# LayerNorm of x + residual on one core: loads two tiles at a time, stores issued by GpSimd instead of ScalarE

## The chip, the core and the metric

The kernel runs on one core of a Trainium2 chip. The engines that matter are VectorE (DVE), ScalarE (ACT), GpSimd (POOL, used here only to issue DMAs) and SyncE (SP, used only to issue DMAs), and the 16 DMA engines that the core's DMA queues share. TensorE does no work. The metric is the device time of one execution in microseconds (us); before the change the median of 4 runs is 265.06 us (264.94 to 265.14).

## The reference

```python
x, residual: (16, 1024, 512) float32    gamma, beta: (512,) float32
z = x + residual
mean = np.mean(z, axis=-1, keepdims=True)
var = np.var(z, axis=-1, keepdims=True)
out = gamma * (z - mean) / np.sqrt(var + eps) + beta
```

These are 16384 rows of 512 numbers. Each of x, residual and the output is 33.55 MB in float32, so that at least 100.7 MB cross the memory interface, whatever the kernel does.

## The kernel before

Each of the 128 partitions holds 128 consecutive rows, and the kernel goes through them in tiles of `_R = 4` rows per partition: a tile is 128 x 4 x 512 numbers, 1 MB in float32. The loop that makes the list of tiles halves the last one, so that there are 31 tiles of four rows and 2 tiles of two rows.

The work on tile i is cut into stages. `emit_loads` brings x by a DMA from SP's queue (tile `zt`) and residual by a DMA from POOL's queue (tile `rt`), which turns it into bf16 on the way. `emit_sums` has DVE add the residual in place and collect the sum of each row (L94, four instructions), and has ACT square the sum and collect the sum of squares (L101, four). `emit_m2`, `emit_var`, `emit_sqrt` and `emit_rstd` are small instructions on 4 numbers per partition, on DVE but for the square root on ACT. `emit_norm` has ACT write (z - mean) / std as bf16 into `ut` (L165, four). `emit_fin` has DVE multiply by gamma (`wt`, L178) and add beta (`ot`, L183), and issues the store of the tile, from ACT's queue (L188).

The main loop is a software pipeline written out by hand: in its turn i it emits the loads up to tile i + 11, the norm of tile i - 4, the sums of tile i, and the end (`emit_fin`) of tile i - 5:

```python
for i in range(n_t + 5):
    for k in range(10):
        emit_loads(i + 2 + k)
    emit_norm(i - 4)
    emit_sqrt(i - 2)
    emit_sums(i)
    emit_m2(i)
    emit_fin(i - 5)
    emit_rstd(i - 3)
    emit_var(i - 1)
```

A scheduler then fixes an order for each engine; each engine takes its instructions in that order, and an instruction that waits holds up all behind it on its engine. The number of buffers sets how far one engine may run ahead of another: 12 tiles for x (`_XB`), 12 for residual (`_RB`), 4 for the output (`_OB`). An x buffer comes free when the norm of its tile is done, a residual buffer when the sums of its tile are done, an output buffer when its store has landed. Beside that, the DMAs that SP and ACT issue share eight semaphores (DMAHW0 to DMAHW7), taken in turn, and those that POOL issues have eight others (DMASW0 to DMASW7): a DMA whose semaphore is still in use waits at its issue until the earlier DMA with it has landed.

Of the kernel before, what the change touches and what calls it, by code (L numbers as in the profile page):

```python
# [7 lines left out]

_R = 4
_XB = 12  # L10
_RB = 12
_OB = 4
_CAST_R = True
_STORE_Q = "act"


@with_exitstack
def kernel(
    ctx: ExitStack,
    tc: tile.TileContext,  # L20
    x: bass.AP,
    residual: bass.AP,
    gamma: bass.AP,
    beta: bass.AP,
    eps: bass.AP,
    out: bass.AP,
):
    nc = tc.nc
    P = nc.NUM_PARTITIONS

    f32 = mybir.dt.float32
    bf16 = mybir.dt.bfloat16
    AT = mybir.ActivationFunctionType
    OP = mybir.AluOpType

    x_f = x.flatten_outer_dims()
    r_f = residual.flatten_outer_dims()
    o_f = out.flatten_outer_dims()
    N, D = x_f.shape
    assert D <= 512  # L40

    inv_d = 1.0 / float(D)
    eps_f = float(eps)

    n_rows = N // P
    tiles = []
    r0 = 0
    while r0 < n_rows:
        rem = n_rows - r0
        R = _R if rem > _R else max(_R // 2, 1)  # L50
        R = min(R, rem)
        tiles.append((r0, R))
        r0 += R
    n_t = len(tiles)

    x_v = x_f.rearrange("(p r) d -> p r d", p=P)
    r_v = r_f.rearrange("(p r) d -> p r d", p=P)
    o_v = o_f.rearrange("(p r) d -> p r d", p=P)

    consts = ctx.enter_context(tc.tile_pool(name="consts", bufs=1))  # L60
    xz = ctx.enter_context(tc.tile_pool(name="xz", bufs=_XB))
    rl = ctx.enter_context(tc.tile_pool(name="rl", bufs=_RB))
    mids = ctx.enter_context(tc.tile_pool(name="mids", bufs=3))
    outs = ctx.enter_context(tc.tile_pool(name="outs", bufs=_OB))
    stats = ctx.enter_context(tc.tile_pool(name="stats", bufs=6))
    junk = ctx.enter_context(tc.tile_pool(name="junk", bufs=1, space=bass.MemoryType.PSUM))

    st = {}

    def emit_loads(i):  # L70
        if i >= n_t or i in st:
            return
        r0, R = tiles[i]
        zt = xz.tile([P, _R, D], f32, name=f"zt{i}", tag="zt")[:, :R]
        nc.sync.dma_start(out=zt, in_=x_v[:, r0 : r0 + R])  # L75
        if _CAST_R:
            rt = rl.tile([P, _R, D], bf16, name=f"rt{i}", tag="rt")[:, :R]
            nc.gpsimd.dma_start(out=rt, in_=r_v[:, r0 : r0 + R])  # L78
        else:
            rt = rl.tile([P, _R, D], f32, name=f"rt{i}", tag="rt")[:, :R]  # L80
            nc.sync.dma_start(out=rt, in_=r_v[:, r0 : r0 + R])
        st[i] = dict(zt=zt, rt=rt)

    sq_junk = junk.tile([P, D], f32, name="sq_junk")

    def emit_sums(i):
        if i >= n_t or i < 0:
            return
        s = st[i]
        r0, R = tiles[i]  # L90
        zt, rt = s["zt"], s["rt"]
        sums = stats.tile([P, _R], f32, name=f"sums{i}", tag="sums")
        for j in range(R):
            nc.vector.scalar_tensor_tensor(  # L94
                out=zt[:, j], in0=zt[:, j], scalar=0.0, in1=rt[:, j],
                op0=OP.add, op1=OP.add,
                accum_out=sums[:, j : j + 1],
            )
        ssq = stats.tile([P, _R], f32, name=f"ssq{i}", tag="ssq")
        for j in range(R):  # L100
            nc.scalar.activation(  # L101
                out=sq_junk, in_=zt[:, j], func=AT.Square,
                accum_out=ssq[:, j : j + 1],
            )
        s["sums"] = sums
        s["ssq"] = ssq

    def emit_m2(i):
        if i >= n_t or i < 0:
            return  # L110
        s = st[i]
        r0, R = tiles[i]
        m2 = stats.tile([P, _R], f32, name=f"m2{i}", tag="m2")
        nc.vector.scalar_tensor_tensor(  # L114
            out=m2[:, :R], in0=s["sums"][:, :R], scalar=-inv_d,
            in1=s["sums"][:, :R], op0=OP.mult, op1=OP.mult,
        )
        s["m2"] = m2

    def emit_var(i):  # L120
        if i >= n_t or i < 0:
            return
        s = st[i]
        r0, R = tiles[i]
        varn = stats.tile([P, _R], f32, name=f"varn{i}", tag="varn")
        nc.vector.tensor_tensor(  # L126
            out=varn[:, :R], in0=s["ssq"][:, :R], in1=s["m2"][:, :R], op=OP.add
        )
        s["varn"] = varn

    def emit_sqrt(i):
        if i >= n_t or i < 0:
            return
        s = st[i]
        r0, R = tiles[i]
        stdv = stats.tile([P, _R], f32, name=f"stdv{i}", tag="stdv")
        nc.scalar.activation(  # L137
            out=stdv[:, :R], in_=s["varn"][:, :R], func=AT.Sqrt, bias=eps_t,
            scale=inv_d,
        )  # L140
        s["stdv"] = stdv

    def emit_rstd(i):
        if i >= n_t or i < 0:
            return
        s = st[i]
        r0, R = tiles[i]
        rstd = stats.tile([P, _R], f32, name=f"rstd{i}", tag="rstd")
        nc.vector.reciprocal(out=rstd[:, :R], in_=s["stdv"][:, :R])  # L149
        cc = stats.tile([P, _R], f32, name=f"cc{i}", tag="cc")  # L150
        nc.vector.scalar_tensor_tensor(  # L151
            out=cc[:, :R], in0=s["sums"][:, :R], scalar=-inv_d, in1=rstd[:, :R],
            op0=OP.mult, op1=OP.mult,
        )
        s["rstd"] = rstd
        s["cc"] = cc

    def emit_norm(i):
        if i >= n_t or i < 0:
            return  # L160
        s = st[i]
        r0, R = tiles[i]
        ut = mids.tile([P, _R, D], bf16, name=f"ut{i}", tag="ut")
        for j in range(R):
            nc.scalar.activation(  # L165
                out=ut[:, j], in_=s["zt"][:, j], func=AT.Identity,
                bias=s["cc"][:, j : j + 1], scale=s["rstd"][:, j : j + 1],
            )
        s["ut"] = ut

    def emit_fin(i):
        if i >= n_t or i < 0:
            return
        s = st[i]
        r0, R = tiles[i]
        ut = s["ut"][:, :R]
        wt = mids.tile([P, _R, D], bf16, name=f"wt{i}", tag="wt")[:, :R]
        nc.vector.tensor_tensor(  # L178
            out=wt, in0=ut, in1=gamma_bf.unsqueeze(1).to_broadcast((P, R, D)),
            op=OP.mult,  # L180
        )
        ot = outs.tile([P, _R, D], f32, name=f"ot{i}", tag="ot")
        nc.vector.tensor_tensor(  # L183
            out=ot[:, :R], in0=wt,
            in1=beta_f.unsqueeze(1).to_broadcast((P, R, D)), op=OP.add,
        )
        eng = nc.scalar if _STORE_Q == "act" else nc.gpsimd
        eng.dma_start(out=o_v[:, r0 : r0 + R], in_=ot[:, :R])  # L188
        del st[i]

    emit_loads(0)
    emit_loads(1)

    gamma_f = consts.tile([P, D], f32)
    nc.sync.dma_start(out=gamma_f, in_=gamma.unsqueeze(0).to_broadcast((P, D)))  # L195
    beta_f = consts.tile([P, D], f32)
    nc.sync.dma_start(out=beta_f, in_=beta.unsqueeze(0).to_broadcast((P, D)))  # L197
    gamma_bf = consts.tile([P, D], bf16)
    nc.vector.tensor_copy(out=gamma_bf, in_=gamma_f)  # L199
    eps_t = consts.tile([P, 1], f32)  # L200
    nc.vector.memset(eps_t, eps_f)  # L201

    for i in range(n_t + 5):
        for k in range(10):
            emit_loads(i + 2 + k)
        emit_norm(i - 4)
        emit_sqrt(i - 2)
        emit_sums(i)
# [4 lines that stand above are left out]
# [35 lines left out]
```

## Time and profile before

| | before |
|---|---|
| median of 4 runs | 265.06 us |
| the profiled execution, its time | 265.22 us |
| its span, first to last instruction | 263.3 us |
| DVE busy | 203.2 us (77%) |
| ACT busy | 182.6 us (69%) |
| POOL busy (issue of DMAs) | 17.8 us (7%) |
| read from memory / written to it | 67.63 MB / 33.55 MB |
| the chain that ended last | DMA 61%, ACT 16%, DVE 13% |

A queue q1 of the profile carries the loads of x (SP), q0 the loads of residual (POOL), and q10 the stores (ACT). The sizes that the profile gives are those of what is written, so that q0 shows half of what it reads: it reads float32 and writes bf16. A chain of waits is read backwards from the last instruction, and its shares say which kind of work the end hung on, not that this work was at its limit the whole time.

### The profile page before, as it was taken

To read this page: it belongs to the slowest core of one execution; us is meant where nothing else is said; L and a number is where in the kernel's file an instruction comes from. 1 tells how busy PE (TensorE), PEld (TensorE's weight loads), DVE (VectorE), ACT (ScalarE), POOL (GpSimd) and SP (SyncE) were. 2 spreads that over 40 slices of the span, in tenths; PEclk is the share of its full clock that TensorE was granted. 3 is DMA by queue.
4 is the path that set the end of the run, shared out by engine and by line. 5 is a ranking of instruction groups with operands and counts; after the bars stand their busy time and mean duration, and the time that the engine had idled before them with its cause. 6 is when DMAs were issued, how large, how long until landed. Compare 5 with 4: busy or idle time off the path is not lost.

```text
span 263.3 us, 1203 instructions
## 1 busy us (share of the span) xinstructions
DVE 203.2 (77%) x456; ACT 182.6 (69%) x419; POOL 17.8 (7%) x37
## 2 busy tenths in 40 slices
DVE  0354696792959998699989878888898589976893
ACT  1386689564354842999987885777770699999950
POOL 6010011000100000000000000000000000000000
DMA  7999999999999999999999999999999998433756
GB/s 251 251 265 313 317 316 340 339 351 349 325 353 321 353 350 327 348 350 352 359 350 347 351 361 350 349 356 355 350 348 356 371 382 355 205 159 159 299 236 261
DMA packets 14552, 84.48 MB, mean 321 GB/s; under 512 B 1616, under 2 KB 1616, under 8 KB 6608
## 3 DMA queue, kind: packets, MB, share of 16 engines
q1 hardware_dynamic: 5040, 34.08, 32.4%
q0 software_dynamic: 4752, 16.78, 31.7%
q10 hardware_dynamic: 4752, 33.56, 30.5%
q14 instruction: 8, 0.07, 0.1%
HBM read 67.63 MB, written 33.55 MB: 384 GB/s over the span
## 4 chain that ended last, share of the span: by engine, by line
DMA 61%; ACT 16%; DVE 13%; issue 7%; ACTq 1%; SPq 1%; DVEq 0%
DMA zt<-in_x_dram 61%; ACT ut L165 8%; ACT sq_junk L101 7%; DVE ot L183 4%; DVE zt L94 4%; DVE wt L178 3%; ACTq L188 1%; ACT stdv L137 1%; DVE varn L126 1%; DVE cc L151 0%; DVE rstd L149 0%; SPq L75 0%; SPq L197 0%; SPq L195 0%; DVE m L114 0%
## 5 line engine op out<-in xcount | busy, mean ns | idle before, releaser
L101 ACT ACTIVATE sq_junk<-zt 128x512 f32<-128x512 f32 x128 | 75.0, 586 | 58.1 <-DVE cc L151 24.8
L94 DVE SCALAR_TENSOR_TENSOR zt<-zt,rt 128x512 f32<-128x512 f32 x128 | 81.4, 688 | 43.8 <-DMA zt<-in_x_dram 32.5
L165 ACT ACTIVATE ut<-zt,cc,rstd 128x512 bf16<-128x512 f32 x128 | 98.7, 799 | 3.3 <-DVE cc L151 3.3
L183 DVE TENSOR_TENSOR ot<-wt,beta_f 128x2048 f32<-128x2048 bf16 (+1 forms) x33 | 73.4, 2225 | 0.1
L178 DVE TENSOR_TENSOR wt<-ut,gamma_bf 128x2048 bf16<-128x2048 bf16 (+1 forms) x33 | 39.2, 1188 | 6.5 <-ACT ut L165 6.3
L78 POOL DMA_DIRECT2D rt<-in_residual_dram x33 | 17.6, 541 | 145.6 <-DMA rt<-in_residual_dram 124.0
L101 ACT ACTIVATION_READ_ACCUMULATOR sq_junk<-zt 128x1 f32 x128 | 23.9, 187 | 0.0
L137 ACT ACTIVATE stdv<-varn,eps_t 128x4 f32<-128x4 f32 (+1 forms) x33 | 9.4, 284 | 7.5 <-DVE varn L126 7.5
L94 DVE DVE_READ_ACCUMULATOR zt<-zt,rt 128x1 f32 x128 | 10.5, 82 | 0.0
L126 DVE TENSOR_TENSOR varn<-ssq,m 128x4 f32<-128x4 f32 (+1 forms) x33 | 5.2, 156 | 3.1 <-ACT sq_junk L101 3.1
L149 DVE RECIPROCAL rstd<-stdv 128x4 f32<-128x4 f32 (+1 forms) x33 | 5.6, 170 | 0.8 <-ACT stdv L137 0.8
L114 DVE SCALAR_TENSOR_TENSOR m<-sums 128x4 f32<-128x4 f32 (+1 forms) x33 | 5.2, 159 | 0.8
L101 ACT ACT_TABLE_LOAD x1 | 1.3, 1283 | 5.7 <-DMA zt<-in_x_dram 5.7
L151 DVE SCALAR_TENSOR_TENSOR cc<-sums,rstd 128x4 f32<-128x4 f32 (+1 forms) x33 | 5.1, 156 | 0.0
L137 ACT ACT_TABLE_LOAD x1 | 1.3, 1283 | 0.0
L201 DVE MEMSET eps_t<- 128x1 f32 x1 | 0.1, 59 | 0.8 <-PEq L229 0.8
L199 DVE CAST gamma_bf<-gamma_f 128x512 bf16<-128x512 f32 x1 | 0.4, 422 | 0.0
L229 POOL MEMSET const-float32-0.0<- 128x1 f32 x1 | 0.1, 99 | 0.2 <-issue 0.2
L229 POOL MEMSET const-bfloat16-1.0<- 128x1 bf16 x1 | 0.1, 102 | 0.0
L229 POOL MEMSET const-float32-1.0<- 128x1 f32 x1 | 0.1, 99 | 0.0
L229 POOL MEMSET const-uint8-127<- 128x1 uint8 x1 | 0.1, 99 | 0.0
## 6 DMA issues: line engine op xcount, KB each, us to landing
zt<-in_x_dram SPq DMA_DIRECT2D x31, 1024.0 KB, 30.5
out_dram<-ot ACTq DMA_DIRECT2D x31, 1024.0 KB, 11.4
rt<-in_residual_dram POOLq DMA_DIRECT2D x31, 512.0 KB, 51.7
zt<-in_x_dram SPq DMA_DIRECT2D x2, 512.0 KB, 25.1
out_dram<-ot ACTq DMA_DIRECT2D x2, 512.0 KB, 2.9
rt<-in_residual_dram POOLq DMA_DIRECT2D x2, 256.0 KB, 56.8
gamma_f<-in_gamma_dram SPq DMA_DIRECT2D x1, 256.0 KB, 12.4
beta_f<-in_beta_dram SPq DMA_DIRECT2D x1, 256.0 KB, 15.6
```

Of the source, the lines that this page charges most:

```text
L78: nc.gpsimd.dma_start(out=rt, in_=r_v[:, r0 : r0 + R])
L94: nc.vector.scalar_tensor_tensor(out=zt[:, j], in0=zt[:, j], scalar=0.0, in1=rt[:, j], op0=OP.add, op1=OP.add, accum_out=sums[:, j : j + 1],)
L101: nc.scalar.activation(out=sq_junk, in_=zt[:, j], func=AT.Square, accum_out=ssq[:, j : j + 1],)
L114: nc.vector.scalar_tensor_tensor(out=m2[:, :R], in0=s["sums"][:, :R], scalar=-inv_d, in1=s["sums"][:, :R], op0=OP.mult, op1=OP.mult,)
L126: nc.vector.tensor_tensor(out=varn[:, :R], in0=s["ssq"][:, :R], in1=s["m2"][:, :R], op=OP.add)
L137: nc.scalar.activation(out=stdv[:, :R], in_=s["varn"][:, :R], func=AT.Sqrt, bias=eps_t, scale=inv_d,)
L149: nc.vector.reciprocal(out=rstd[:, :R], in_=s["stdv"][:, :R])
L151: nc.vector.scalar_tensor_tensor(out=cc[:, :R], in0=s["sums"][:, :R], scalar=-inv_d, in1=rstd[:, :R], op0=OP.mult, op1=OP.mult,)
L165: nc.scalar.activation(out=ut[:, j], in_=s["zt"][:, j], func=AT.Identity, bias=s["cc"][:, j : j + 1], scale=s["rstd"][:, j : j + 1],)
L178: nc.vector.tensor_tensor(out=wt, in0=ut, in1=gamma_bf.unsqueeze(1).to_broadcast((P, R, D)), op=OP.mult,)
L183: nc.vector.tensor_tensor(out=ot[:, :R], in0=wt, in1=beta_f.unsqueeze(1).to_broadcast((P, R, D)), op=OP.add,)
L188: eng.dma_start(out=o_v[:, r0 : r0 + R], in_=ot[:, :R])
```

## The change

The code loads x and residual for two tiles with one DMA each (`_GX = 2`, `_GR = 2`), 2 MB from memory instead of 1 MB. There are 5 such buffers for x (10 tiles, before 12) and 4 for residual (8 tiles, before 12). The output keeps a DMA for each tile, but has 8 buffers instead of 4, and its store is issued from POOL's queue. All 32 tiles have four rows; the two half tiles are gone. The list of loads reaches to tile i + 13 in turn i. The arithmetic is the same, instruction for instruction, but for the two half tiles.

```diff
-_R = 4
-_XB = 12
-_RB = 12
-_OB = 4
+_RC = 4
+_GX = 2
+_GR = 2
+_GO = 1
+_XB = 5
+_RB = 4
+_OB = 8
-_STORE_Q = "act"
+_STORE_Q = "pool"
...
+    def emit_xload(g):
...
+        R = _GX * _RC
+        t = xz.tile([P, R, D], f32, name=f"xg{g}", tag="xg")
+        nc.sync.dma_start(out=t, in_=x_v[:, g * R : (g + 1) * R])
+        xg[g] = t
+
+    def emit_rload(g):
...
+        R = _GR * _RC
+        t = rl.tile([P, R, D], bf16 if _CAST_R else f32, name=f"rg{g}", tag="rg")
+        eng = nc.gpsimd if _CAST_R else nc.sync
+        eng.dma_start(out=t, in_=r_v[:, g * R : (g + 1) * R])
+        rg[g] = t
...
+            st[i] = dict(
+                zt=xg[i // _GX][:, (i % _GX) * _RC : (i % _GX) * _RC + _RC],
+                rt=rg[i // _GR][:, (i % _GR) * _RC : (i % _GR) * _RC + _RC],
+            )
...
-        eng = nc.scalar if _STORE_Q == "act" else nc.gpsimd
-        eng.dma_start(out=o_v[:, r0 : r0 + R], in_=ot[:, :R])
+        if i % _GO == _GO - 1 or i == n_t - 1:
+            R = _GO * _RC
+            eng = nc.gpsimd if _STORE_Q == "pool" else nc.scalar
+            n_done = (i % _GO) + 1
+            eng.dma_start(
+                out=o_v[:, g * R : g * R + n_done * _RC],
+                in_=og[g][:, : n_done * _RC],
+            )
...
-        for k in range(10):
-            emit_loads(i + 2 + k)
+        for k in range(2, 2 + 12):
+            emit_loads(i + k)
```

What this does to the engines' orders is seen at three places. In these rows a name carries its tile or group number and behind it a serial number: `zt17` is x of tile 17, `xg7` is x of tiles 14 and 15, `rg8` is residual of tiles 16 and 17, `og4` is the output of tile 4; `sq_junk` is the unused result of a square, `stdv` the result of a square root. The brackets tell the semaphores that an instruction waits for.

On ACT before, in the middle of the program, the store of tile 12 stands between the first and the second square of tile 17, and the rest of tile 17's squares and the norm of tile 14 stand behind it:

```order
L137 ACTIVATE stdv15_653<-varn15_642,eps_t_91 128x4 [waits DVE_49]
L101 ACTIVATE sq_junk_76,ssq17_660<-zt17_270 128x512 [waits DMAHW7_49,Activation_49]
L188 DMA out_0_dram<-ot12_669 128x2048 [waits DMAHW0_49,DVE_49]
L101 ACTIVATE sq_junk_76,ssq17_660<-zt17_270 128x512 [waits Activation_49]
L165 ACTIVATE ut14_682<-zt14_183,cc14_674,rstd14_672 128x512 [waits DVE_49]
L101 ACTIVATE sq_junk_76,ssq17_660<-zt17_270 128x512 [waits Activation_49]
```

On ACT now there are no stores left: a tile is four squares, four norms and a square root in a row.

```order
L142 ACTIVATE stdv11_473<-varn11_462,eps_t_87 128x4 [waits DVE_49]
L111 ACTIVATE sq_junk_76,ssq13_480<-xg6_109 128x512 [waits DVE_49,Activation_49] x4
L167 ACTIVATE ut10_498<-xg5_105,cc10_494,rstd10_492 128x512 [waits DVE_49]
L167 ACTIVATE ut10_498<-xg5_105,cc10_494,rstd10_492 128x512 x3
L142 ACTIVATE stdv12_503<-varn12_496,eps_t_87 128x4 [waits DVE_49]
```

ACT no longer waits for DVE's output or for a DMA semaphore at a store. POOL, which before had 33 loads of residual in a row and nothing else, now has each load of a pair and then two stores, here in the middle of the program:

```order
L81 DMA rg8_161<-in_residual_dram 128x4096 [waits DMASW4_49,DVE_49]
L195 DMA out_0_dram<-og4_359 128x2048 [waits DMASW5_49,DVE_49]
L195 DMA out_0_dram<-og5_389 128x2048 [waits DMASW6_49,DVE_49]
L81 DMA rg9_210<-in_residual_dram 128x4096 [waits DMASW7_49,DVE_49]
L195 DMA out_0_dram<-og6_423 128x2048 [waits DMASW0_49,DVE_49]
L195 DMA out_0_dram<-og7_453 128x2048 [waits DMASW1_49,DVE_49]
L81 DMA rg10_274<-in_residual_dram 128x4096 [waits DMASW2_49,DVE_49]
```

So the stores have moved behind and between the loads of residual on one queue, with one set of eight semaphores for both. On SP the loads of x stand alone; the first that waits for a buffer is the sixth:

```order
L72 DMA xg0_77<-in_x_dram 128x4096
L205 DMA gamma_f_81<-in_gamma_dram 128x512
L207 DMA beta_f_83<-in_beta_dram 128x512
L72 DMA xg1_89<-in_x_dram 128x4096
L72 DMA xg2_93<-in_x_dram 128x4096
L72 DMA xg3_97<-in_x_dram 128x4096
L72 DMA xg4_101<-in_x_dram 128x4096
L72 DMA xg5_105<-in_x_dram 128x4096 [waits DMAHW0_49,DVE_49,Activation_49]
```

Before, SP issued 33 loads of 1 MB there; now it issues 16 of 2 MB, with no store of ACT's between them in the turn of the semaphores.

More of the change, by code (lines that the diff above doesn't have):

```diff
@@ L45 @@
     n_rows = N // P
[L46 to L54, printed above, removed]
+    n_t = n_rows // _RC
+    assert n_rows % _RC == 0
     x_v = x_f.rearrange("(p r) d -> p r d", p=P)
@@ L66 @@
     junk = ctx.enter_context(tc.tile_pool(name="junk", bufs=1, space=bass.MemoryType.PSUM))
+    xg, rg, og = {}, {}, {}
     st = {}
+    def emit_xload(g):
+        if g * _GX >= n_t or g in xg:
+            return
+        R = _GX * _RC
[3 more added lines that the diff above has]
+    def emit_rload(g):
+        if g * _GR >= n_t or g in rg:
+            return
+        R = _GR * _RC
[3 more added lines that the diff above has]
+        rg[g] = t
     def emit_loads(i):
-        if i >= n_t or i in st:
+        if i >= n_t:
             return
[L73 to L82, printed above, removed]
+        emit_xload(i // _GX)
+        emit_rload(i // _GR)
+        if i not in st:
+            st[i] = dict(
+                zt=xg[i // _GX][:, (i % _GX) * _RC : (i % _GX) * _RC + _RC],
+                rt=rg[i // _GR][:, (i % _GR) * _RC : (i % _GR) * _RC + _RC],
+            )
     sq_junk = junk.tile([P, D], f32, name="sq_junk")
@@ L89, in emit_sums @@
         s = st[i]
-        r0, R = tiles[i]
         zt, rt = s["zt"], s["rt"]
-        sums = stats.tile([P, _R], f32, name=f"sums{i}", tag="sums")
-        for j in range(R):
+        sums = stats.tile([P, _RC], f32, name=f"sums{i}", tag="sums")
+        for j in range(_RC):
             nc.vector.scalar_tensor_tensor(
@@ L98, in emit_sums @@
             )
-        ssq = stats.tile([P, _R], f32, name=f"ssq{i}", tag="ssq")
-        for j in range(R):
+        ssq = stats.tile([P, _RC], f32, name=f"ssq{i}", tag="ssq")
+        for j in range(_RC):
             nc.scalar.activation(
@@ L111, in emit_m2 @@
         s = st[i]
-        r0, R = tiles[i]
-        m2 = stats.tile([P, _R], f32, name=f"m2{i}", tag="m2")
+        m2 = stats.tile([P, _RC], f32, name=f"m2{i}", tag="m2")
         nc.vector.scalar_tensor_tensor(
-            out=m2[:, :R], in0=s["sums"][:, :R], scalar=-inv_d,
-            in1=s["sums"][:, :R], op0=OP.mult, op1=OP.mult,
+            out=m2, in0=s["sums"], scalar=-inv_d, in1=s["sums"],
+            op0=OP.mult, op1=OP.mult,
         )
@@ L123, in emit_var @@
         s = st[i]
[L124 to L128, printed above, removed]
+        varn = stats.tile([P, _RC], f32, name=f"varn{i}", tag="varn")
+        nc.vector.tensor_tensor(out=varn, in0=s["ssq"], in1=s["m2"], op=OP.add)
         s["varn"] = varn
@@ L134, in emit_sqrt @@
         s = st[i]
-        r0, R = tiles[i]
-        stdv = stats.tile([P, _R], f32, name=f"stdv{i}", tag="stdv")
+        stdv = stats.tile([P, _RC], f32, name=f"stdv{i}", tag="stdv")
         nc.scalar.activation(
-            out=stdv[:, :R], in_=s["varn"][:, :R], func=AT.Sqrt, bias=eps_t,
-            scale=inv_d,
+            out=stdv, in_=s["varn"], func=AT.Sqrt, bias=eps_t, scale=inv_d
         )
@@ L146, in emit_rstd @@
         s = st[i]
[L147 to L150, printed above, removed]
+        rstd = stats.tile([P, _RC], f32, name=f"rstd{i}", tag="rstd")
+        nc.vector.reciprocal(out=rstd, in_=s["stdv"])
+        cc = stats.tile([P, _RC], f32, name=f"cc{i}", tag="cc")
         nc.vector.scalar_tensor_tensor(
-            out=cc[:, :R], in0=s["sums"][:, :R], scalar=-inv_d, in1=rstd[:, :R],
+            out=cc, in0=s["sums"], scalar=-inv_d, in1=rstd,
             op0=OP.mult, op1=OP.mult,
@@ L161, in emit_norm @@
         s = st[i]
-        r0, R = tiles[i]
-        ut = mids.tile([P, _R, D], bf16, name=f"ut{i}", tag="ut")
-        for j in range(R):
+        ut = mids.tile([P, _RC, D], bf16, name=f"ut{i}", tag="ut")
+        for j in range(_RC):
             nc.scalar.activation(
```

16 lines of the change are left out of this document (9 added, 7 removed).

## The prediction

> **What bounds the kernel now.** I read the page's slices first, then the queues, then stages by windows, then the chain and ACT's waits. From the page (busy us and share of each engine; the slices; the queues; the bytes):
>
> ```profile
> DVE 203.2 (77%) x456; ACT 182.6 (69%) x419; POOL 17.8 (7%) x37
> DMA  7999999999999999999999999999999998433756
> q1 hardware_dynamic: 5040, 34.08, 32.4%
> q0 software_dynamic: 4752, 16.78, 31.7%
> q10 hardware_dynamic: 4752, 33.56, 30.5%
> HBM read 67.63 MB, written 33.55 MB: 384 GB/s over the span
> ```
>
> The 16 DMA engines are busy for 94.7% of the span, and full in every slice but the first and the last seven. So the middle has one limit, the DMA engines, and only the two ends can give anything. How fast they go when full is read from the queues between 130 and 200 us:
>
> ```profile
> q1 hardware_dynamic: 1349, 9.86, 34.7%
> q0 software_dynamic: 1351, 4.92, 34.7%
> q10 hardware_dynamic: 1352, 9.90, 33.6%
> ```
>
> q0 reads twice what it writes, so 9.86 + 9.84 + 9.90 = 29.6 MB pass in 70 us: 423 GB/s, shared in three equal parts. All 101.2 MB at that rate take 239 us. The stages at the end (columns: us, DVE busy, ACT busy, POOL busy, clock, DMA share, GB/s):
>
> ```profile
> 206.00:221.60 15.60, 13.06 (x29) 15.04 (x35) 0.00 (x0) 1.00 0.98 370
> 221.60:245.00 23.40, 18.96 (x34) 23.24 (x54) 0.00 (x0) 1.00 0.50 207
> 245.00:261.50 16.50, 13.26 (x15) 9.24 (x16) 0.00 (x0) 1.00 0.69 283
> 140.00:180.00 40.00, 33.62 (x77) 29.99 (x70) 2.12 (x4) 1.00 1.03 353
> ```
>
> Full is a share of 1.03 (last row). Against it the three stages leave 15.6 x 0.05/1.03 + 23.4 x 0.53/1.03 + 16.5 x 0.34/1.03 = 0.8 + 12.0 + 5.4 = 18.2 us of DMA time unused. With the same start and no gap, the last byte would land at 261.5 - 18.2 = 243.3 us. That is the floor while the rate stays. Why the end has gaps, from the chain and from ACT's timeline:
>
> ```profile
> 176.34 29.70 DMA zt<-in_x_dram
> 206.11 0.34 ACTq L188
> ...
> 228.90 0.72 ACT sq_junk L101 x2
> 234.50 0.72 ACT sq_junk L101 x2
> ```
>
> ```profile
> 195.87 0.18 ACT L101 ACTIVATION_READ_ACCUMULATOR sq_junk<-zt 128x1 f32 x1
> 206.11 0.34 ACTq L188 DMA_DIRECT2D out_dram<-ot  x1
> 206.50 0.60 ACT L101 ACTIVATE sq_junk<-zt 128x512 f32<-128x512 f32 x1 [10.44 <-DMA zt<-in_x_dram]
> ```
>
> ACT stands for 10.4 us in front of a store, which goes out only when a load of x issued at 176.34 has landed, because both use the same semaphore. Squares that could run are queued behind it. From then on ACT is the limit: 15.04 of 15.6 us and 23.24 of 23.4 us busy, one tile each 5.60 us (228.90 to 234.50), and the stores trickle at 1 MB per 5.6 us through engines that can do 2.4 MB.
>
> **The change, part by part.** *Stores off ACT.* ACT loses 33 issues and their waits; what it does per tile stays 5.6 us, below DVE's:
>
> ```profile
> 128.74 2.24 DVE ot L183
> 135.11 2.24 DVE ot L183
> ```
>
> DVE needs 6.37 us a tile when nothing is late, so 12.74 us a pair; the DMA engines need 6.29 MB / 423 = 14.9 us a pair. ACT is then never last in steady state, DVE has 2.1 us to spare, and DMA stays the limit of the middle.
>
> *Who is late next.* Residual and stores now share one queue in a fixed order: load g, then stores 2g-12 and 2g-11, load g+1, and so on. While DVE waits for load g, it has done the sums to tile 2g-1 and the ends to tile 2g-6, so the loads to g+3 and the stores between them are ready: up to eight DMAs, some 11 MB, wait on POOL's queue. It doesn't run dry, and a store there doesn't wait for DVE in front of a load. x has five buffers; load g+3 goes out after the norm of tile 2g-1, about 9 us after residual g landed (a turn of 6.4 us and a norm of 2.9 us), and at half the rate (two queues share evenly, as three did above) takes 2.1 MB / 0.21 = 10 us. So x is early and residual is late. I put the smaller depth (10 and 8 tiles for 12 and 12) at nothing: the full POOL queue hides it.
>
> *Start.* Below, the first sum of before and POOL's first issues, from the timeline, and between them all that the DMA engines did in the first 5 us, from the queues of that window.
>
> ```profile
> 10.73 0.69 DVE L94 SCALAR_TENSOR_TENSOR zt<-zt,rt 128x512 f32<-128x512 f32 x1 [9.87 <-DMA rt<-in_residual_dram]
> q1 hardware_dynamic: 148, 1.14, 65.4%
> 1.23 4.37 POOL L78 DMA_DIRECT2D rt<-in_residual_dram  x8 [0.79 <-PEq L243]
> ```
>
> Residual begins after 5 us, though issued at 1.23. A first pair of 2 MB at half rate lands at about 5 + 10 = 15 us, 4.5 us later than before. DVE has time (203 us busy in all), the queues hold 18.9 MB without any buffer coming back, 44 us of work: nothing on the path.
>
> *The end.* Count back from the floor. When residual pair 12 (tiles 24, 25) lands, what remains is residual 13 to 15 (6.3 MB), x 15 and about 0.9 MB of x 14 (3.0 MB), and stores 12 to 31 (21.0 MB): 30.3 MB or 71.5 us, so it lands at 243.3 - 71.5 = 171.8. The next three land 15, 27 and 37 us after it, since x runs out and POOL's queue has the engines to itself. DVE now is slower than that: its pairs start at 0, 15 (waiting), 27.7 and 40.5, so tiles 30 and 31 start at 171.8 + 40.5 = 212.3. From there two turns of 6.37 us, then five ends alone. In the timeline of before an end alone takes DVE (the second column is its duration)
>
> ```profile
> 248.04 1.23 DVE L178 TENSOR_TENSOR wt<-ut,gamma_bf 128x2048 bf16<-128x2048 bf16 x1 [0.68 <-ACT ut L165]
> 251.58 1.22 DVE L178 TENSOR_TENSOR wt<-ut,gamma_bf 128x2048 bf16<-128x2048 bf16 x1
> 248.10 2.92 ACT L165 ACTIVATE ut<-zt,cc,rstd 128x512 bf16<-128x512 f32 x4
> ```
>
> 3.54 us, with ACT's 2.92 us of norm beside it: 12.74 + 5 x 3.6 = 30.7, last output at 243.0. Its store is 1 MB, not 0.5. On ACT's idle queue that took 3.9 us (DMA issues from 220 us on: KB each, median us to landing; then the last issues in the timeline, and POOL's issues with least, median and longest ns):
>
> ```profile
> out_dram<-ot ACTq DMA_DIRECT2D x8, 1024.0 KB, 3.9
> 257.09 2.38 ACTq L188 DMA_DIRECT2D out_dram<-ot  x2
> L78 POOL DMA_DIRECT2D rt<-in_residual_dram x33: 530/530/664, 1.2 to 163.1; - x33
> ```
>
> POOL's issue is 0.53 us; how long its queue then needs to begin no row shows alone. It is 3.9 us in all at best, and 3.8 us more at worst (issued at 1.23, nothing before 5); The queue is running at that point, so I stay near the best case and take 1.4 of the 3.8: 0.5 + 5.3 = 5.8, between 4.4 and 8.2. Last landing 248.8. Before, the last store was issued at 259.1 (257.09 + 2.38 - 0.34) and the window to 261.5 holds its transfer, so that the program ended about 263.3 - 261.5 = 1.8 after it; the profiled execution took 265.22 for a span of 263.3, 1.9 more, and is 0.16 above the median, which I leave out. 248.8 + 1.8 + 1.9 = 252.5 us. Stores do not hold this up: at 212 us some eight are queued, and 14 of them at 2.5 us each end with the floor.
>
> *The rest.* One tile fewer saves DVE five instructions of this kind, 0.8 us, inside its slack:
>
> ```profile
> L126 DVE TENSOR_TENSOR varn<-ssq,m 128x4 f32<-128x4 f32 (+1 forms) x33 | 5.2, 156 | 3.1 <-ACT sq_junk L101 3.1
> ```
>
> POOL issues 48 DMAs at 0.53 us, 25 us in all, beside the transfers. Pieces of 16 KB for each partition instead of 8 KB: no row has them; the two full rates seen, 418 and 423 (the first is quoted under A), differ by 1.2%, so I bound the effect by 1.2% of 239 us, 2.9 us either way, and take 0, since nothing says which way.
>
> *A rule beside a row.* The start of POOL's queue stands above as at most 3.8 us late, by its first DMA. The Trainium skill, "DMA: Bandwidth & Descriptors", section "Specifications", gives a first-byte latency of about 1 us to a GpSimd DMA and about 0.6 us to one of SyncE or ScalarE. By it the last store would take 0.4 us more than on ACT's queue, 4.8 us in place of my 5.8, and the sum would be 251.5; by the row's worst case it would be 254.9. The row is of a queue that starts cold with eight DMAs issued at once, the page's of one DMA.
>
> **The rivals.**
> *A. POOL's queue alone can't fill the engines (slower).* It carries two thirds of the bytes and is alone for 4.9 us of each pair, some 12 pairs, and for about 18 us after x has ended: 77 us on the path. For it: no row of before shows it alone. Beside x between 5 and 20 us it had
>
> ```profile
> q0 software_dynamic: 495, 1.83, 63.6%
> q1 hardware_dynamic: 512, 2.17, 39.7%
> 3.00:5.00 2.00, 0.00 (x0) 0.00 (x0) 2.00 (x4) 1.00 1.02 418
> ```
>
> 3.66 MB in 15 us, 244 GB/s, which is the lower bound. Against it: that is what x left, and SP's queue alone reached 418 (last row), the upper one. I take 420. At 364 the 77 us become 89.5 and the gain is gone; at 300 the time is 284. The Trainium skill, "DMA: Bandwidth & Descriptors", section "Bandwidth", gives 425 GB/s for a GpSimd load of 16 MB and 341 for one of 1 MB; by the latter this kernel would come to 271, by the former to the forecast.
> *B. DMA never idle to the end.* If DVE isn't behind at tiles 30 and 31, the floor holds: 243.3 + 1 + 1.8 + 1.9 = 248. For it: 2.1 us of slack a pair; against it, the last three pairs come faster than DVE takes them.
> *C. It doesn't do what it says.* The end stays paced by 5.6 us a tile, because ACT is behind for another reason than the store (squares and norms are all its work): 11 us come back and the time is 263 to 265.5. For it, ACT also waits elsewhere (us in total, times, longest):
>
> ```profile
> ACT sq_junk L101 <- DVE cc L151: 24.8, 12, 4.2
> ACT sq_junk L101 <- DMA zt<-in_x_dram: 23.2, 3, 10.4
> ```
>
> Against: with no store in its order it holds 5.6 us against DVE's 6.37.
>
> **How the numbers follow.** Forecast as summed, 249 to 257: 0.52. B, 245 to 249: 0.16. A in a mild form, 257 to 264.5: 0.14; A beyond its break-even: 0.11. C: 0.07, of which 0.05 within 0.2% of 265.06 (0.2%, 0.5 us, is about what a measurement tells from no change) and 0.02 below. So faster 0.84, same 0.05, slower 0.11. The range 245.5 to 262.5 leaves out A beyond its break-even (0.11), C (0.07) and the upper end of mild A (0.02).
>
> **What would show it.** Right: no wait of ACT for a DMA in front of squares; DMA share near 1.03 until about 230 us; DVE waiting for residual, not x; last residual landing near 209; first sum near 15 us; ends 3.6 us apart in the last 20 us. Wrong: a DMA share below 1 in the middle while only POOL's queue has work (A), ACT over 95% busy from 205 us (C), or a gap between the last output and the last landing of more than 7 us.

## The result, and the profile after

| | before | after |
|---|---|---|
| median (lowest to highest) | 265.09 us (264.93 to 265.47, 12 runs) | 249.02 us (248.81 to 250.25, 8 runs) |
| ratio, 95% interval | | 0.9402 [0.9388, 0.9416] |
| profiled execution: time, span | 265.22, 263.3 us | 249.12, 247.4 us |

The changed kernel is 16.1 us faster. The page of after: busy time of the engines, the DMA slices, queues (packets, MB, share of the 16 engines), bytes, and the chain.

```profile
DVE 196.0 (79%) x450; ACT 189.1 (76%) x418; POOL 25.9 (10%) x52
DMA  7999999999999999999999999999999999999774
q0 software_dynamic: 6912, 50.33, 64.8%
q1 hardware_dynamic: 2592, 34.08, 33.1%
HBM read 67.63 MB, written 33.55 MB: 409 GB/s over the span
DMA 66%; issue 23%; DVE 4%; POOL 3%; SPq 1%; POOLq 0%; DVEq 0%
```

The slices are where the time came from. Before, the last seven read 8433756, now the last three read 774. The middle was full and is full. The queues' shares give the engines' work: before 32.4 + 31.7 + 30.5 = 94.6% of 263.3 us, 249 us; now 97.9% of 247.4, 242 us. So 7 us of engine time went too. Some 5 of them come with the longer pieces of the loads, as the experiment with single loads shows; where the rest went isn't shown. The waits of after (us in total, times, longest):

```profile
DVE xg L104 <- DMA rg<-in_residual_dram: 25.4, 6, 13.3
ACT ut L167 <- DVE cc L154: 17.1, 8, 5.2
DVE xg L104 <- DMA xg<-in_x_dram: 15.8, 3, 10.1
ACT sq_junk L111 <- DVE xg L104: 13.2, 4, 7.3
ACT L111 <- DMA xg<-in_x_dram: 10.4, 1, 10.4
```

DVE now waits for data of both kinds and for nothing else that matters. Its waits for x all end by 52 us; from 140 us on it waits for residual alone. The wait of 10.4 us in the last row is the first tile's at the start; the waits of before that stood in front of a store are gone. The end in stages (us, DVE busy, ACT busy, POOL busy, clock, DMA share, GB/s):

```profile
206.00:220.00 14.00, 14.00 (x33) 13.65 (x30) 1.06 (x2) 1.00 1.01 424
220.00:230.00 10.00, 10.00 (x17) 8.90 (x19) 1.06 (x3) 1.00 0.99 416
230.00:240.00 10.00, 9.93 (x7) 5.56 (x8) 1.59 (x3) 1.00 0.73 302
240.00:245.50 5.50, 0.16 (x1) 0.00 (x0) 0.53 (x1) 1.00 0.56 232
```

Up to 230 us both DVE and the DMA engines are full; only then does DVE alone set the pace. The last x landed at 190.8 us and the last residual at 207.3. From 208 to 220 us only stores are left, all on POOL's queue, and they fill the engines:

```profile
q0 software_dynamic: 700, 5.10, 100.9%
DMA packets 701, 5.11 MB, mean 426 GB/s; under 512 B 77, under 2 KB 77, under 8 KB 77
```

### The profile page after: what moved, and what is told of

Its sections match the earlier page's. It is cut to its first block, busy times and chain, and to the rows that moved or that the text cites. A ratio compares the mean times of both kernels' runs of the same rounds, so it can differ in the third digit from the quotient of the medians.

```text
span 247.4 us, 1190 instructions
## 1 busy us (share of the span) xinstructions
DVE 196.0 (79%) x450; ACT 189.1 (76%) x418; POOL 25.9 (10%) x52
## 4 chain that ended last, share of the span: by engine, by line
DMA 66%; issue 23%; DVE 4%; POOL 3%; SPq 1%; POOLq 0%; DVEq 0%
DMA out_dram<-og 31%; DMA xg<-in_x_dram 20%; DMA rg<-in_residual_dram 16%; POOL out_dram L195 3%; DVE xg L104 2%; DVE og L187 1%; DVE wt L183 1%; SPq L72 1%; POOLq L253 0%; POOL rg L81 0%; SPq L205 0%; SPq L207 0%; DVE cc L154 0%; POOLq L195 0%; DVE varn L134 0%
## 5 line engine op out<-in xcount | busy, mean ns | idle before, releaser
L104 DVE SCALAR_TENSOR_TENSOR xg<-xg,rg 128x512 f32<-128x512 f32 x128 | 81.1, 687 | 41.2 <-DMA rg<-in_residual_dram 25.4
L167 ACT ACTIVATE ut<-xg,cc,rstd 128x512 bf16<-128x512 f32 x128 | 95.0, 801 | 18.2 <-DVE cc L154 17.1
L111 ACT ACTIVATE sq_junk<-xg 128x512 f32<-128x512 f32 x128 | 76.0, 594 | 17.3 <-DVE xg L104 13.2
L187 DVE TENSOR_TENSOR og<-wt,beta_f 128x2048 f32<-128x2048 bf16 x32 | 72.5, 2265 | 0.1
L183 DVE TENSOR_TENSOR wt<-ut,gamma_bf 128x2048 bf16<-128x2048 bf16 x32 | 39.0, 1220 | 0.0
L195 POOL DMA_DIRECT2D out_dram<-og x32 | 17.0, 532 | 140.9 <-DVE varn L134 66.4
L111 ACT ACTIVATION_READ_ACCUMULATOR sq_junk<-xg 128x1 f32 x128 | 23.8, 186 | 0.0
L81 POOL DMA_DIRECT2D rg<-in_residual_dram x16 | 8.7, 545 | 73.9 <-DVE rstd L152 25.2
L104 DVE DVE_READ_ACCUMULATOR xg<-xg,rg 128x1 f32 x128 | 10.5, 82 | 0.0
L142 ACT ACTIVATE stdv<-varn,eps_t 128x4 f32<-128x4 f32 x32 | 8.9, 282 | 0.6 <-DVE varn L134 0.6
L111 ACT ACT_TABLE_LOAD x1 | 1.3, 1283 | 10.4 <-DMA xg<-in_x_dram 10.4
```

Of the source, the lines that this page charges most:

```text
L81: eng.dma_start(out=t, in_=r_v[:, g * R : (g + 1) * R])
L104: nc.vector.scalar_tensor_tensor(out=zt[:, j], in0=zt[:, j], scalar=0.0, in1=rt[:, j], op0=OP.add, op1=OP.add, accum_out=sums[:, j : j + 1],)
L111: nc.scalar.activation(out=sq_junk, in_=zt[:, j], func=AT.Square, accum_out=ssq[:, j : j + 1],)
L142: nc.scalar.activation(out=stdv, in_=s["varn"], func=AT.Sqrt, bias=eps_t, scale=inv_d)
L167: nc.scalar.activation(out=ut[:, j], in_=s["zt"][:, j], func=AT.Identity, bias=s["cc"][:, j : j + 1], scale=s["rstd"][:, j : j + 1],)
L183: nc.vector.tensor_tensor(out=wt, in0=ut, in1=gamma_bf.unsqueeze(1).to_broadcast((P, _RC, D)), op=OP.mult,)
```

## The experiments

Each ratio is to the kernel before, in runs on the same chip.

### Which part of the change carries it

**Stores on POOL's queue, nothing else.** The kernel before with one word changed:

```diff
-_STORE_Q = "act"
+_STORE_Q = "pool"
```

> The kernel before with one edit: its stores go out from POOL's queue instead of ACT's; loads, tile sizes and buffers stay (12, 12 and 4 tiles). Theory 1 (the place of the store: ACT stood in front of it and the DMA engines ran dry at the end): most of the gain is here, 250 to 254 us, with the DMA engines full until about 235 us. Rival 2 (the transfers of two tiles each are what helped, by longer pieces and fewer issues): 262 to 266 us. Rival 3 (8 output buffers are what lets stores lag behind and fill the end): with 4 buffers the DMA engines still run dry, 258 to 264 us.

Measured: 276.51 us, 1.0432 [1.0416, 1.0447], outside all three ranges. The move alone costs 11.4 us. Its waits and its DMA slices:

```profile
DVE ot L183 <- DMA out_dram<-ot: 46.9, 14, 28.3
DVE zt L94 <- DMA rt<-in_residual_dram: 11.2, 2, 9.9
DMA  7999999999999999999999999999999334443773
220.00:240.00 20.00, 20.00 (x49) 19.48 (x42) 1.59 (x3) 1.00 0.46 191
```

DVE waits 46.9 us for an output buffer, once 28.3 us: the store that would free it stands on POOL's queue behind a dozen tiles of residual. At the end (last row, columns as above) the loads are done, DVE is busy for the whole 20 us with tiles that lay ready, and the engines are half empty.

**The same with fewer residual buffers.** On top of the last one, so 12 buffers for x and 4 each for residual and output:

```diff
-_RB = 12
+_RB = 4
```

> The kernel before with its stores on POOL's queue, 4 output buffers, and only 4 residual buffers instead of 12: a resource taken away from the run that was 276.5 us. Theory 'depth' (on one queue in a fixed order the loads of residual may run no more tiles ahead than there are output buffers, or DVE waits for a store that lies behind those loads): the wait of L183 for stores, 46.9 us there, falls below 10 us and the time to 249 to 258 us. Rival 'four buffers are too few, or POOL's queue is slow for stores': 265 to 280 us, since less room can't help.

Measured: 258.60 us, 0.975 [0.9736, 0.9765]. The wait did what the theory 'depth' said, and the time is just above its range; its rival, by which less room can't help, is out. Eight buffers *less* than in the run above make it 17.9 us faster. DVE's wait for output falls from 46.9 to 8.9 us, and it waits for residual instead:

```profile
DVE ot L183 <- DMA out_dram<-ot: 8.9, 10, 1.2
DVE zt L94 <- DMA rt<-in_residual_dram: 30.5, 13, 9.7
```

**The changed kernel with 4 output buffers.**

```diff
-_OB = 8
+_OB = 4
```

> The changed kernel with 4 output buffers instead of 8. Theory 1 alone, with the stores' lag not needed: 249 to 250 us. Rival 3: DVE waits for output buffers while stores queue behind loads of residual, 253 to 262 us, and in the trace DVE's L187 waits for stores.

Measured: 264.05 us, 0.9969 [0.9956, 0.9982]. Of 16.1 us, 15.0 are gone: theory 1 alone is out, and rival 3 had the wait right and its size too small. Its wait and its slices:

```profile
DVE og L187 <- DMA out_dram<-og: 26.0, 11, 3.7
DMA  7999999999999999999999999999999996434773
```

**The changed kernel with 2 residual buffers (4 tiles).**

```diff
-_RB = 4
+_RB = 2
```

> The changed kernel with 2 residual buffers (4 tiles) instead of 4: stores on POOL's queue and 8 output buffers stay, but the loads of residual run only 4 tiles ahead, so that stores lie behind fewer of them. 'Lag': fewer stores are left at the end of the loads, 255 to 262 us, the DMA engines half idle from about 220 us. Theory 'eight buffers and POOL's queue are enough': 249 to 252 us.

Measured: 258.76 us, 0.977 [0.9742, 0.9798], as 'lag' said. Eight output buffers and POOL's queue are not enough either. No wait for output shows now; residual takes its place, with 46.5 us against 25.4:

```profile
DVE xg L104 <- DMA rg<-in_residual_dram: 46.5, 13, 13.2
```

**The changed kernel with single loads.** Same tiles of buffer, no pairs:

```diff
-_GX = 2
-_GR = 2
+_GX = 1
+_GR = 1
-_XB = 5
-_RB = 4
+_XB = 10
+_RB = 8
```

> The changed kernel with loads of one tile each (1 MB of x, 1 MB of residual), 10 and 8 such buffers, which is the same room; stores from POOL, 8 output buffers. Theory 1: 249 to 253 us; what the pairs are worth is the difference to 249.0. If the longer pieces for each partition (16 KB instead of 8 KB) make the DMA engines faster by the 1.3% by which the changed kernel's engines finished earlier than my floor, 252 us. Rival 2: 260 to 266 us.

Measured: 249.67 us, 0.9418 [0.9403, 0.9434], against 249.02. The pairs are worth 0.65 us at the medians, which is less than the runs of after differ among themselves (248.81 to 250.25). The engines' work is back at 65.8 + 33.9 = 99.7% of a span of 248.0 us, 247 us, but with no gap at the end:

```profile
q0 software_dynamic: 9216, 50.34, 65.8%
q1 hardware_dynamic: 4896, 34.08, 33.9%
DMA  7999999999999999999999999999999999999990
```

**What these five say together.** From the records of the transfers' completions and of DVE's instructions, I counted for each kernel, at 190 us, the tiles whose residual has landed but that DVE has not yet summed, and the tiles that DVE has finished but whose store has not landed. "Lead" is the residual buffers in tiles, "out" the output buffers. (In two kernels a half tile counts as one.)

| kernel | lead, out | landed, not summed | finished, not stored | last sum starts | time |
|---|---|---|---|---|---|
| stores on POOL alone | 12, 4 | 8 | 4 | 248.8 | 276.51 |
| after with 4 outputs | 8, 4 | 2.75 | 4 | 233.3 | 264.05 |
| stores on POOL, lead 4 | 4, 4 | 0.5 | 4 | 231.1 | 258.60 |
| after with lead 4 | 4, 8 | 0 | 2 | 227.1 | 258.76 |
| after, single loads | 8, 8 | 1 | 7 | 216.2 | 249.67 |
| after | 8, 8 | 1 | 7 | 218.4 | 249.02 |

Work left for the end can lie in two places. A tile in a load buffer still costs DVE a turn of 6 us; a tile in an output buffer costs the DMA engines 2.5 us, beside DVE's last tiles. A fixed order of loads and stores on one queue decides which: a lead greater than the output buffers leaves DVE behind, waiting for a store; a small lead leaves no heap of finished tiles that wait for their stores. Only a lead and output buffers that are about equal, and both large, put the heap behind DVE. (The tiles that have landed and are not summed are about lead minus out: 8 for 12 and 4, some 3 for 8 and 4, one or none where the lead is no greater.) Windows from the last sum to the last landing, of after, of after with 4 outputs and of after with a lead of 4:

```profile
218.38:244.30 25.92, 21.71 (x27) 16.09 (x29) 3.19 (x6) 1.00 0.85 352
```

```profile
233.27:259.20 25.93, 21.73 (x27) 16.09 (x29) 3.19 (x6) 1.00 0.66 273
```

```profile
227.14:253.00 25.86, 21.71 (x27) 16.09 (x29) 3.19 (x6) 1.00 0.66 274
```

All three take 25.9 us from the last sum to the last byte. So the time follows when that sum starts: 14.9 us later with 4 outputs (15.0 in the medians), 8.8 with a lead of 4 (9.7; its profiled execution was 0.9 us below its median). In after 25.9 us x 352 GB/s = 9.1 MB are left for this stretch, in the others 7.1. With single loads the stretch takes 28.1 us, since the engines stay full to the end of it; in the two kernels that end on half tiles it takes 21.9.

### Was it ACT that emptied the end?

**The changed kernel with its stores on ACT.**

```diff
-_STORE_Q = "pool"
+_STORE_Q = "act"
```

> The changed kernel with one edit undone: its stores go out from ACT's queue again; pairs and buffers stay. Theory 1: the waits of ACT in front of stores come back and with them the empty end, 259 to 266 us. Rival 2: 248 to 251 us. Rival 3: 249 to 254 us, since the 8 output buffers are there.

Measured: 266.97 us, 1.0072 [1.0055, 1.009]. Pairs and eight output buffers are worth nothing on ACT's queue. The Trainium skill, "DMA: Bandwidth & Descriptors", section "SWDGE vs HWDGE vs iDMA", gives plain transfers, as this store is, to SP or ACT. With the old buffers the runs agree (265.1 on ACT, 276.5 on POOL), with the new ones they don't (267.0 and 249.0). SP waits before loads of x, and ACT before squares, for a store:

```profile
SPq L72 <- DMA out_dram<-og: 47.7, 4, 15.8
ACT sq_junk L111 <- DMA out_dram<-og: 12.5, 2, 10.8
220.00:240.00 20.00, 17.21 (x29) 18.36 (x44) 0.00 (x0) 1.00 0.40 165
```

**The same, each store one turn later,** so that DVE's output is ready when ACT comes to it:

```diff
-    for i in range(n_t + 5):
+    for i in range(n_t + 7):
...
+        emit_store(i - 6)
```

> The changed kernel with its stores on ACT's queue, each issued one turn of the loop later, so that ACT never stands in front of a store whose data isn't ready (267.0 us without that delay). Theory 'place' (what costs is ACT waiting for DVE's output in the middle of its squares): 249 to 255 us. Rival 'shared semaphores' (what costs is that SP's loads of x wait for stores that use the same eight semaphores, 47.7 us in that run): 260 to 267 us, with SP waiting for stores as before.

Measured: 264.46 us, 0.9968 [0.9954, 0.9983], 2.5 us less: 'place' is out, and the time lies where 'shared semaphores' put it. SP's wait is still 39.0 us; ACT's wait for stores, 14.6 us, is no shorter than before.

**Each store four turns later,** `emit_store(i - 9)`.

> The changed kernel with its stores on ACT's queue, each issued four turns of the loop after its data is ready (264.5 us with one turn), 8 output buffers. Theory 'lag' (what counts is that stores are held back while loads run, so that the loads are done early and a heap of stores is left to fill the end; POOL's queue does that by its order, and the 8 buffers allow it): with four turns more left over, 252 to 258 us. Theory 'ACT's queue itself' (its waits for semaphores shared with SP, whenever the stores are issued): 262 to 267 us.

Measured: 265.46 us (263.57 to 266.50), 1.0016 [0.9991, 1.0041]: not 'lag', but the range of 'ACT's queue itself'. SP's wait for stores is down to 3.0 us, so that it isn't the semaphores shared with SP that hold the time there. Behind its first tile ACT waits for no DMA any more, and the engines are still half empty from 205 to 240 us, and full after it:

```profile
205.00:220.00 15.00, 14.82 (x36) 13.55 (x31) 0.00 (x0) 1.00 0.46 188
220.00:240.00 20.00, 15.80 (x25) 19.24 (x45) 0.00 (x0) 1.00 0.51 208
240.00:262.00 22.00, 13.58 (x12) 8.59 (x13) 0.00 (x0) 1.00 0.90 371
```

The heap is there, but ACT's own order holds it back until its squares and norms are done. The run doesn't test what a heap is worth.

**Three turns late to tile 20, then tiles 21 to 23 at once, then one turn late.**

```diff
+        if i < 29:
+            emit_store(i - 8)
+        elif i == 29:
+            emit_store(21)
+            emit_store(22)
+            emit_store(23)
+        else:
+            emit_store(i - 6)
```

> The changed kernel with its stores on ACT's queue, each issued three turns after its data is ready up to tile 20, and those held back then issued together when the last loads are being used; from tile 24 on one turn late. In the run with four turns all the way (265.5 us) the loads of x were done at 206 us, 9 us earlier than without the delay, but the stores in hand waited for their place in ACT's order and the DMA engines stood half idle from 205 to 240 us. 'Lag' (held-back stores fill the end, on whatever queue): 252 to 258 us. 'ACT's queue itself' (its order ties stores, squares and norms together, and its semaphores tie them to loads of x): 261 to 267 us.

Measured: 261.10 us, 0.9851 [0.9832, 0.9871]. A heap that is let go when the loads end helps on ACT's queue too, by 3.4 us against one turn late. That is about half of the least that 'lag' had expected, and the time is at the lower edge of what 'ACT's queue itself' said. What is left at the end:

```profile
200.00:220.00 20.00, 19.79 (x45) 17.90 (x41) 0.00 (x0) 1.00 0.68 280
220.00:240.00 20.00, 16.39 (x28) 19.84 (x47) 0.00 (x0) 1.00 0.73 302
SPq L72 <- DMA out_dram<-og: 21.8, 2, 15.3
DVE og L187 <- DMA out_dram<-og: 10.0, 3, 5.8
```

From 220 us ACT is busy 19.84 of 20 us, with stores between its squares and norms: in these kernels ACT is the bound of the end, as the prediction read it before. SP still waits 21.8 us for stores.

**Stores on ACT with semaphores of their own.** The loads of x move to POOL's queue, so that stores alone use the semaphores of SP's and ACT's queues:

```diff
-        nc.sync.dma_start(out=t, in_=x_v[:, g * R : (g + 1) * R])
+        nc.gpsimd.dma_start(out=t, in_=x_v[:, g * R : (g + 1) * R])
```

> The changed kernel with its stores on ACT's queue, in the place where they cost 267.0 us, and the loads of x moved to POOL's queue, so that the stores have their semaphores to themselves. 'Shared semaphores': 249 to 257 us. 'Place': 261 to 268 us, and ACT still stands in front of stores. Both parts: in between. x and residual now share one queue, which could cost by itself.

Measured: 274.29 us, 1.0341 [1.0323, 1.0359]. It doesn't answer its question, because x, which waits for a norm before a buffer is free, now holds residual back on the same queue:

```profile
POOL rg L81 <- DVE varn L134: 80.2, 6, 24.2
POOL xg L72 <- ACT stdv L142: 69.9, 10, 17.3
```

**What the runs with stores on ACT have in common.** The switch of the queue did more than move the stores: with it the scheduler gave ACT and DVE another order for the same arithmetic. In all eight kernels with stores on POOL, ACT takes four squares and then four norms. In all six with stores on ACT it takes squares and norms mixed, as shown above for before. When the last sum starts, the POOL kernels still have 4 squares, 17 norms and 6 ends to do (2, 15 and 6 with half tiles), the ACT kernels 13 squares, 26 or 27 norms and 8 ends (12, 25 and 8 in before). Windows from the last sum to the last landing, of the run with 261.10 us, of before, and of before with its stores on POOL (these two end on half tiles):

```profile
220.67:257.73 37.06, 29.73 (x38) 28.29 (x58) 0.00 (x0) 1.00 0.76 311
227.10:261.40 34.30, 26.80 (x38) 27.02 (x56) 0.00 (x0) 1.00 0.60 245
248.78:270.60 21.82, 18.33 (x27) 13.05 (x23) 3.35 (x7) 1.00 0.71 288
```

With the old buffers, moving the stores to POOL makes this stretch 12.5 us shorter (34.3 to 21.8), and the last sum starts 21.7 us later. With the new ones the stretch is 12.6 us shorter (38.5 to 25.9), and the last sum starts 6.9 us earlier. So the move is worth some 12.5 us at the end either way, and the buffers decide what it does before the end. Of the 12 us between the run with 261.10 us and after, 2.3 lie before the last sum and 11.2 behind it, less 1.5 by which the span of after runs on longer behind its last landing. Behind the last sum all loads have landed (by 209.2 us), and neither ACT nor DVE waits for a DMA there. So the waits of SP for stores aren't what makes this part long. No run has the one order of the arithmetic with the other queue, and none puts the stores on SP's queue; how much of the 12.5 us is the order, and how much the stores' place on ACT, isn't shown.

### Past the change

**One residual pair more, one x pair less, nine outputs.**

```diff
-_XB = 5
-_RB = 4
-_OB = 8
+_XB = 4
+_RB = 5
+_OB = 9
```

> An attempt at a better one: the changed kernel with the room shared out otherwise, 4 pairs of x (5), 5 pairs of residual (4), 9 output buffers (8). If DVE's late last pairs are what is left (its last output at 240.2 us, while the DMA engines could have ended near 240), residual that runs further ahead brings 246 to 248.5 us. If the rule 'residual no further ahead than there are output buffers' binds (10 tiles against 9), DVE waits for stores and it is 249.5 to 254 us.

Measured: 248.44 us, 0.9367 [0.9353, 0.9382], just inside the first range. A lead one tile greater than the output buffers doesn't bind: DVE waits for an output buffer for 3.5 us in all. Its last sum starts 6.4 us before that of after, with nine finished tiles not stored at 190 us, and yet it is only 0.6 us faster:

```profile
211.97:243.60 31.63, 21.72 (x27) 16.09 (x29) 3.19 (x6) 1.00 0.90 381
220.00:240.00 20.00, 13.69 (x12) 8.55 (x12) 2.65 (x5) 1.00 1.00 422
```

12.0 MB are left after its last sum, more than pass in 25.9 us; the engines are full until 240 us, and DVE is no longer what ends it. That is the floor of rival B.

**Stores of 2 MB, but for the last six tiles.** Four output buffers of two tiles:

```diff
-_GO = 1
+_GO = 2
-_OB = 8
+_OB = 4
...
+        if i >= n_t - 6:
+            eng.dma_start(out=o_v[:, i * _RC : (i + 1) * _RC], in_=ot)
+        elif i % _GO == _GO - 1:
...
```

> An attempt at a better one: the changed kernel with one store of 2 MB for each pair (4 buffers of two tiles), single stores for the last six tiles. The busy time of the DMA engines fell from 248.0 to 241.7 us when the pieces of x and residual became 16 KB; if 16 KB pieces save the same for stores, some 2 us, and the end stays as it is, 247 to 248.5 us; if DVE's late end is the only limit, 249 us; if pairs of output hold back the stores too long, 250 to 254 us.

Measured: 247.54 us (247.49 to 247.61), 0.9348 [0.9331, 0.9364], the fastest of all, 1.5 us below after and inside the first range. The reason given for it holds in part: the engines' busy time fell by 0.8 us (242.2 to 241.4), not by 2. The last sum starts 1.1 us earlier than in after (217.3), the stretch behind it is the same 25.8 us, and the span ends 0.5 us sooner after the last landing.

## Why the prediction was right, step by step

The forecast was 252.5 us, the median is 249.02. The frame held. A POOL queue that can't fill the engines (A) is out: stores alone went at 426 GB/s, and with a load among them, between the last packets of residual pairs 14 and 15 (197.52 and 207.32 us), a pair and two stores passed, 4.19 MB in 9.80 us or 428 GB/s. The engines are full to 230 us, as forecast, and what ends the program is DVE's last tiles and one store.

**The sum.** These rows of after's timeline carry it:

```profile
14.18 0.69 DVE L104 SCALAR_TENSOR_TENSOR xg<-xg,rg 128x512 f32<-128x512 f32 x1 [13.31 <-DMA rg<-in_residual_dram]
206.85 1.23 DVE L183 TENSOR_TENSOR wt<-ut,gamma_bf 128x2048 bf16<-128x2048 bf16 x1
210.47 0.69 DVE L104 SCALAR_TENSOR_TENSOR xg<-xg,rg 128x512 f32<-128x512 f32 x1
212.92 1.22 DVE L183 TENSOR_TENSOR wt<-ut,gamma_bf 128x2048 bf16<-128x2048 bf16 x1
...
237.87 2.29 DVE L187 TENSOR_TENSOR og<-wt,beta_f 128x2048 f32<-128x2048 bf16 x1
240.46 0.53 POOL L195 DMA_DIRECT2D out_dram<-og  x1 [2.93 <-DVE og L187]
```

| step | forecast | measured | difference |
|---|---|---|---|
| first sum | 15 | 14.18 | not on the path |
| tile 30 starts | 212.3 | 210.47 | -1.8 |
| from there to the last output | 30.7 | 240.16 - 210.47 = 29.7 | -1.0 |
| last output to its landing | 5.8 | 244.24 - 240.16 = 4.1 | -1.7 |
| landing to end of span | 1.8 | 247.35 - 244.24 = 3.1 | +1.3 |
| outside the span | 1.9 | 249.02 - 247.35 = 1.7 | -0.2 |

Unrounded, the differences make -3.5. (The last row takes the median less the profiled span; the profiled execution is 0.1 us above the median.) The end of the last transfer, 244.24, is from the transfers' records. By them the last residual landed at 207.3 (forecast 208.8), and pairs 13 to 15 came 13.4, 28.0 and 37.8 us after pair 12 (15, 27 and 37). Pair 12 itself landed at 169.5 us, 2.3 us before the forecast's 171.8, and that is where the -1.8 comes from; why it was early isn't shown. The +1.3 is the longer end of the span, also without a known reason. The terms that were mis-sized:

- *A turn of DVE* took 212.92 - 206.85 = 6.07 us, not 6.37; two turns make 0.6 of the 1.0. DVE now starts `wt` when the sums end. Before, two small instructions stood between (timeline of before), so `wt` started 0.27 us after the last row of the sums:

```profile
133.54 0.08 DVE L94 DVE_READ_ACCUMULATOR zt<-zt,rt 128x1 f32 x1
133.65 0.16 DVE L114 SCALAR_TENSOR_TENSOR m<-sums 128x4 f32<-128x4 f32 x1
133.81 1.22 DVE L178 TENSOR_TENSOR wt<-ut,gamma_bf 128x2048 bf16<-128x2048 bf16 x1
```

- *The last store* took 4.1 us from the last output to its last packet, not 5.8. Counted from its issue to its semaphore, as the 3.9 on ACT's queue was, it took 4.1 us too, some 0.2 more than on ACT's queue, and POOL's issue alone is 0.2 longer (0.53 us against 0.34). The 1.4 us that I added for a queue that starts late were wrong: here the queue had been running. The sum also counted some 0.3 us twice, since its 3.9 us end at the semaphore and its 1.8 us begin at the last packet. The Trainium skill, "DMA: Bandwidth & Descriptors", section "Specifications", would have put 0.4 us more there than for ACT's, and is nearer than I was.
- *16 KB pieces*, put at 0 within 2.9 us either way, took some 5 us off the engines' work (247.4 us with single loads, 242.2 in after). On the path they are worth no more than 0.65 us.

**The steps that failed** are two statements about the cause. *Stores off ACT* was named as what fills the end. Behind the last sum that is borne out, by 12.5 us with either set of buffers. But the step put it down to the issues and waits of the stores, and the order of ACT's and DVE's work changed with the queue too. The runs that put the stores later in ACT's order gain 2.5, 1.5 and 5.9 us of the 18.0 between 266.97 and 249.02. And the step took the move to be a gain by itself; with the old buffers it costs 11.4 us, because DVE is held back before the end. *"I put the smaller depth (10 and 8 tiles for 12 and 12) at nothing"* was read with the doubled output as given. Residual's depth and the output buffers together are what decides: 8 and 8 give 249.0, 8 and 4 give 264.05, 12 and 4 give 276.5. The doubled output was in the change and had no price in the sum, though "some eight" queued stores in the step *The end* were only possible by it; that is 15.0 us. The total came out since the count back to tile 30 assumed that DVE runs right behind residual, which these buffers make true. No step had argued that they fit each other, so in this the right number was luck.

Rival C said that ACT would bound the end whatever the store does. It is wrong for the change and half right as a reading: with stores on ACT and its waits for DMAs gone, ACT is still busy for 19.24 of 20 us.

**Open:** of the 12.5 us behind the last sum, how much is the order of ACT's and DVE's work and how much the stores' place on ACT's queue; and of the 1.3 to 6.9 us by which the last sum starts later than in after in the four runs with stores on ACT and x on SP, how much are semaphores that these two queues share. The run meant for that had a new wait of its own.

## What to carry to other kernels

Loads and stores that share a queue in a fixed order need a lead of loads that is not much greater than the output buffers (10 against 9 tiles cost nothing here, 8 against 4 cost 15.0 us), and both deep enough that finished tiles, not loaded ones, are what lies waiting when the loads end. Look at whether a moved DMA also changed the order of the arithmetic on the engine that it left. Before pricing a store that moves, write down what will stand ahead of it on the new queue, in bytes, and how many output buffers bridge that. When the DMA engines are full in the middle, compare kernels by the start of the last tile's work and by the bytes left at that time: in the kernels with stores on POOL and no half tiles what follows took 25.8 to 25.9 us, whatever came before, until those bytes no longer fit.

## What the runs showed of the hardware

- The span goes on after the last landing. Where ACT stores last it is 1.6 us (16 or 32 DMAs on POOL) or 1.9 (33, in before). Where POOL stores last it is the longer the more DMAs POOL issued: 2.6 us with 35, 3.1 with 48, 3.8 to 3.9 with 64 or 66. Why isn't shown. It accounts for 0.5 of the 1.5 us that stores of 2 MB gain.
- POOL's queue moved its first bytes some 4 us after its first issue in both kernels, but its last store, 1 MB, had landed 4.1 us after its issue, against 3.9 on ACT's queue.
- In all eight kernels with stores on POOL DVE is busy for 196.0 to 198.4 us and ACT for 188.8 to 190.4; in the six with stores on ACT, before among them, DVE for 200.2 to 203.2 and ACT for 181.8 to 183.9. The arithmetic is the same but for the half tiles. The two groups are also those of the two orders of squares, norms and sums; whether the order is the reason isn't shown.
